# S5's sample end states and rotation tables made ahead of the S5 loop

## The chip, the cores and the metric

The kernel runs on one core of a Trainium2 chip. The metric is device time in microseconds (us) of one execution, as the median of several runs. The engines are TensorE (PE; its weight loads are PEld), VectorE (DVE), ScalarE (ACT), GpSimd (POOL) and SyncE (SP), which here issues all DMAs. Each works through its own queue of instructions in a fixed order, and an instruction that waits holds up everything behind it in its queue.

## The reference

One step of a decoder layer for a prompt of 512 tokens and a sample group of 8 sequences with 4 tokens each, width 1024, all in float32. After an RMSNorm, one projection feeds four branches: Mamba-2 SSD, S5 (a diagonal complex state space model), mLSTM, and cross-attention into 256 memory tokens. Each branch is projected down, weighted with a gate computed from the normed input, and summed; an output projection, a residual and a last norm follow.

What matters here is S5. It has 64 channel groups of 16 channels, each with a complex state of 64 values. With lam = exp(A dt) per state value,

    h[t] = lam * h[t-1] + B u[t],    y[t] = Re(C h[t]) + D u[t]

The prompt starts from h = 0. Each sample sequence starts from its own state h0, and its end state after four tokens is an output: lam^4 h0, plus what the four tokens add.

## The kernel before, in words

All large matmuls go through `unit` (L186 issues the matmuls): a 1024 x 128 slice of weights is loaded as `raw`, ScalarE rounds it to `whi` (L175), VectorE makes the rest `wlo` (L64, the line of all tensor_tensor operations), and TensorE adds up three products for eight blocks, 48 matmuls over 544 columns (512 prompt and 32 sample tokens). Their PSUM tile `pu` has two buffers; all other PSUM tiles share four banks, the tag "bk".

The order of work around the change is this.

- **Attention heads.** A generator `heads_` makes the prompt's attention for four heads, in eight steps: scores `psc` against the keys `krow`, softmax `prb`, transposes `ppt`, values `ppv`, and the branch's gate `zz`. The keys of head h lie in the tile `kst[h]`, which is not needed after the head's scores. A loop over the eight sample sequences b advances `heads_` by one step (`step(hd)`) and the S5 set-up `s5_setup` by two (`step(su, 2)`). Then POOL makes `pmx`, the sample's attention weights masked to sequence b, two loads bring `vb`, and TensorE adds into `pacc` (L675).
- **S5 set-up.** `s5_setup` is a generator with fourteen stops. It makes the powers of lam (`pwr`, `pwi`), the powers `pw8` for the rotations, the scaled B (`bbr`, `bbi`), the transposed C (`ctr`, `cti`) and the transposed states `h0`. Its scratch lies in the tile `merged`, which has no other use yet (`mflat` is its flat view).
- **Rotation tables.** For every two blocks of the loop, q = 0 to 3, `s5_rot(q)` makes on POOL the 64 powers of a unit complex number by doubling: two memsets, and in six rounds six elementwise operations on two halves, 36 operations on 8 to 256 columns, each needing the one before. The result goes to the first 512 columns of `st{q}`, a tile that shares its place with `kst[q]`. Table 0 is made after the heads, with scratch in `mflat`; tables 1 to 3 in the S5 loop after the blocks 0, 2 and 4, with scratch `rt` from the tags "sc1" and "sc2".
- **S5 loop.** For f = 0 to 7, 128 channels each: `s5_scan(f)` multiplies the inputs `U` by `bt` into two PSUM banks `pvr` and `pvi` (72 columns for each of four state blocks: 64 chunks of the prompt and 8 sample sequences), rotates by the table `E`, scans (L811, L812), rotates back, and copies the states into `hs`. At its end stand the end states of the samples, `hn`: lam^4 h0 by six operations on DVE for 32 columns, and two additions of the last eight columns of `pvr` and `pvi`. `s5_mats(f+1)` makes the next block's tables `bm` and `cm` on DVE and POOL, with scratch `q` in single buffers of the tags "sc1" and "sc2"; `s5_mats2(f+1)` transposes `bm` (`pbt`), multiplies to `pk` (L772) and sends the result through DRAM (`kd`, `tp`). `s5_y(f)` makes the outputs `py`, sends `yj` to DRAM (`yd`) and reads it back as `yt`; `s5_out` applies the GELU in the next round. `s5_in(f+2)` makes the inputs; its `uf` shares a buffer with `yj`. Steps of the generator `gate_down` put units on TensorE in between.
- **After the loop**, `hp` and `hn` are transposed (`pho`, `phq`) and written out.

The framework that builds the program fixes each engine's order at build time by the order of the code and by modelled times, and puts in the waits. So an instruction can stand earlier in its queue than in the code: of the six operations on `hn`, the first products of all eight blocks run before the loop, from 250.6 to 252.7 us.

Of the kernel before, what the change touches and what calls it, by code (L numbers as in the profile page):

```python
# [8 lines left out]
F32 = mybir.dt.float32  # L9
# [5 lines left out]
MUL, ADD, SUB, MAX, MIN = ALU.mult, ALU.add, ALU.subtract, ALU.max, ALU.min  # L15
# [19 lines left out]
def hybrid_kernel(ctx: ExitStack, tc: tile.TileContext, I, O):  # L35
# [12 lines left out]
    def bank(name="bk"):  # L48
        return pst.tile([P, 512], F32, name=name, tag="bk")

    def bc(ap, axis, n):
        ap = ap.unsqueeze(axis)
        shape = list(ap.shape)
        shape[axis] = n
        return ap.to_broadcast(shape)
# [7 lines left out]
    def tt(eng, out, a, b, op):  # L63
        eng.tensor_tensor(out, a, b, op)  # L64
# [4 lines left out]
    def cmul(e1, e2, outr, outi, ar, ai, br, bi, t1, t2):  # L69
        tt(e1, outr, ar, br, MUL)  # L70
        tt(e2, t1, ai, bi, MUL)
        tt(e1, outr, outr, t1, SUB)
        tt(e2, outi, ar, bi, MUL)
        tt(e1, t2, ai, br, MUL)
        tt(e2, outi, outi, t2, ADD)
# [158 lines left out]
    def step(gen, n=1):  # L234
        for _ in range(n):
            next(gen, None)
# [297 lines left out]
    def s5_setup():  # L534
# [102 lines left out]
            S.copy(h0[:, ri].rearrange("p b a -> p (b a)"), ph[:, 0:256])  # L637

        yield
        pd = bank("pd")  # L640
        T.transpose(pd[:, 0:8], sdg, ident[0:8, 0:8])
        V.tensor_copy(dcol, pd[:, 0:8])
# [2 lines left out]
    hd = heads_()  # L645
    pacc = pst.tile([P, 512], F32, name="pacc4", tag="bk")

    def s5_rot(q):
        er, ei = ev_[q][:, 0], ev_[q][:, 1]
        G.memset(er[:, :, :, 0:1], 1.0)  # L650
        G.memset(ei[:, :, :, 0:1], 0.0)
        for m in range(6):
            n = 1 << m
            if q < 1:
                ts_ = [mflat[:, (2 * q + i) * 256:(2 * q + i) * 256 + 8 * n] for i in range(2)]
            else:
                ts_ = [s5r.tile([P, 8 * n], F32, name="rt", tag=t) for t in ("sc1", "sc2")]
            t1, t2 = (t.rearrange("p (f a k) -> p f a k", f=2, a=4) for t in ts_)
            wm = tuple(bc(pw8[:, ri, m, 8 * q:8 * q + 8].rearrange("p (f a) -> p f a", a=4), 3, n) for ri in range(2))
            cmul(G, G, er[:, :, :, n:2 * n], ei[:, :, :, n:2 * n], er[:, :, :, 0:n], ei[:, :, :, 0:n], *wm, t1, t2)  # L660

    su = s5_setup()
    for b in range(NB):
        step(hd)
        step(su, 2)
        pm = xv.tile([P, 8, TS], F32, name="pmx", tag="qmx")
        tt(G, pm, pts.rearrange("p m (h t) -> p (m h) t", h=4), bc(bmask[:, b, :], 1, 8), MUL)
        vbs = []
        for m in range(2):
            vb = xv.tile([P, D], F32, name="vb", tag="vb")  # L670
            dma(vb, I["cache_mem_v"][0, b, m * P:(m + 1) * P].rearrange("p h d -> p (h d)"))
            vbs.append(vb)
        for m in range(2):
            for h in range(4):
                T.matmul(pacc[32 * h:32 * h + 32, 0:256], pm[:, 4 * m + h, :], vbs[m][:, h * 256:(h + 1) * 256],  # L675
                         start=b == 0 and m == 0, stop=b == 7 and m == 1, tile_position=(0, 32 * h))
    step(hd, 16)
    step(su, 4)
    stp = [cst.tile([P, 2, NT], F32, name=f"st{q}", tag=f"st{q}") for q in range(4)]
    stag = [stp[i // 2][:, i % 2] for i in range(NK)]  # L680

    ev_ = [t[:, :, 0:512].rearrange("p f (r a k) -> p r f a k", r=2, a=4) for t in stp]
    for q in range(1):
        s5_rot(q)
    os2 = xv.tile([P, 256], F32, name="os2", tag="pss", bufs=1)
    V.tensor_copy(os2, pacc[:, 0:256])
    pb = bank("pxo")
# [100 lines left out]
    def s5_scan(f, U, bt, E):  # L788
# [16 lines left out]
        tt(G, gr, gr, t1, ADD)  # L805
        tt(V, gi, E[:, 0], vi, MUL)
        tt(V, t2, E[:, 1], vr, MUL)
        tt(G, gi, gi, t2, SUB)
        for a in range(4):
            rb = rho8[:, 4 * f + a:4 * f + a + 1].to_broadcast([P, 64])  # L810
# [16 lines left out]
        for g2 in range(2):  # L827
# [2 lines left out]
            S.copy(hsv[64:128, :, g2, 9:73], t3[pr])  # L830
            for ri in range(2):
                S.copy(hsv[64 * ri:64 * ri + 64, :, g2, 0:8], h0[pr, ri, :, gs].rearrange("p b a -> p a b"))
        V.tensor_copy(hp[:, 8 * f:8 * f + 8], hs_[:, :, 72])

        p4 = (bc(pwr[:, 4, gs], 1, NB), bc(pwi[:, 4, gs], 1, NB))
        t1 = s5r.tile([P, NB, 4], F32, name="s1", tag="t1")
        t2 = s5r.tile([P, NB, 4], F32, name="s2", tag="t2")
        hnr, hni = hn[:, 0, :, gs], hn[:, 1, :, gs]
        cmul(V, V, hnr, hni, *p4, h0[:, 0, :, gs], h0[:, 1, :, gs], t1, t2)
        tt(V, hnr, hnr, vv[0][:, :, 64:72].rearrange("p a b -> p b a"), ADD)  # L840
        tt(V, hni, hni, vv[1][:, :, 64:72].rearrange("p a b -> p b a"), ADD)
        return hs_

    def s5_y(f, U, cm, tp, hs_):
# [38 lines left out]
    for f in range(8):  # L883
        bt, cm, tp, E = mt_
        hs_ = s5_scan(f, us_[f], bt, E)
        if f < 7:
            ma = s5_mats(f + 1)
        if f > 0:
            s5_out(f - 1, yt)
        step(gd)  # L890
        if f < 6:
            us_.append(s5_in(f + 2))
        if f < 7:
            mt_ = s5_mats2(f + 1, *ma)
        step(gd, (0, 1, 1, 1, 1, 0, 1, 1)[f])
        yt = s5_y(f, us_[f], cm, tp, hs_)
        if f % 2 == 0 and f // 2 + 1 in range(1, 4):
            s5_rot(f // 2 + 1)
    s5_out(7, yt)

    ph = bank("pho")
# [860 lines left out]
```

## Time and profile before

| | |
|---|---|
| Runs | 1478.04, 1473.43, 1478.48 us; median 1478.04 |
| Profiled execution | 1477.78 us, span 1476.0 us, mean granted clock 0.976 |
| Busy | PE 1397.2, PEld 1335.3, DVE 865.3, ACT 535.8, POOL 335.7 us |
| Attention heads with the set-up | about 157 to 255 us |
| S5 loop and its end | about 255 to 495 us |

Times in the profile count from the start of the span. A line of the profile names the code line, the engine, the operation, the output and inputs, and in brackets how long the engine had been idle before it and what ended that. A wait for several things is put down to the one that came last by the profile, which can be wrong. The granted clock is the share of TensorE's full clock that it was given.

### The profile page before, as it was taken

To read this page: it belongs to the slowest core of one execution; us is meant where nothing else is said; L and a number is where in the kernel's file an instruction comes from. 1 tells how busy PE (TensorE), PEld (TensorE's weight loads), DVE (VectorE), ACT (ScalarE), POOL (GpSimd) and SP (SyncE) were. 2 spreads that over 40 slices of the span, in tenths; PEclk is the share of its full clock that TensorE was granted. 3 is DMA by queue.
4 is the path that set the end of the run, shared out by engine and by line. 5 is a ranking of instruction groups with operands and counts; after the bars stand their busy time and mean duration, and the time that the engine had idled before them with its cause. 6 is when DMAs were issued, how large, how long until landed. Compare 5 with 4: busy or idle time off the path is not lost. (4 is left out here: it accounts for less than half of the span.)

```text
span 1476.0 us, 28630 instructions
## 1 busy us (share of the span) xinstructions
PE 1397.2 (95%) x11713; PEld 1335.3 (90%) x11713; DVE 865.3 (59%) x1682; ACT 535.8 (36%) x945; POOL 335.7 (23%) x511
## 2 busy tenths in 40 slices
PE   6999998979779899999999999999999999899997
PEld 6998887878768799999999989999999998789997
DVE  5455496676776594677777534544343465454553
ACT  4254233554445532433333422423233332114232
POOL 3010133676473011002222222000000011110222
PEclk9999999989989999999999999999999999999999
DMA  8577362545545323323222455222322235663341
GB/s 205 165 211 236 103 200 73 123 113 127 121 103 124 105 72 90 86 75 84 66 80 74 126 167 139 58 79 70 82 72 79 73 111 178 198 194 115 101 147 61
DMA packets 298884, 172.96 MB, mean 117 GB/s; under 512 B 46749, under 2 KB 289769, under 8 KB 298754
## 3 DMA queue, kind: packets, MB, share of 16 engines
q1 hardware_dynamic: 298754, 171.14, 42.1%
q8 instruction: 92, 1.51, 0.4%
q14 instruction: 38, 0.31, 0.1%
HBM read 145.35 MB, written 25.24 MB: 116 GB/s over the span
## 5 line engine op out<-in xcount | busy, mean ns | idle before, releaser
L186 PE MATMUL pu<-xh,whi 128*128 128x272 f32 (+1 forms) x2000 | 427.3, 292 | 0.2 <-DVE hp L949 0.2
L186 PE MATMUL pu<-xl,whi 128*128 128x272 f32 (+1 forms) x2000 | 425.6, 291 | 0.1
L186 PE MATMUL pu<-xh,wlo 128*128 128x272 f32 (+1 forms) x2000 | 425.1, 291 | 0.0
L64 DVE TENSOR_TENSOR wlo<-raw,whi 128x1024 fp32r<-128x1024 f32 x181 | 250.6, 1385 | 224.7 <-ACT whi L175 218.8
L175 ACT CAST whi<-raw 128x1024 fp32r<-128x1024 f32 x181 | 198.6, 1097 | 448.3 <-PE pu L186 343.7
L186 PEld LDWEIGHTS pu<-xh,whi 128*128 128x128 f32 x2000 | 319.0, 190 | 5.8 <-issue 3.9
L186 PEld LDWEIGHTS pu<-xl,whi 128*128 128x128 f32 x2000 | 319.4, 190 | 4.0 <-issue 3.3
L186 PEld LDWEIGHTS pu<-xh,wlo 128*128 128x128 f32 x2000 | 317.7, 190 | 3.3 <-issue 2.9
L186 PE MATMUL pu<-oh,whi 128*128 128x272 f32 x640 | 138.8, 298 | 5.8 <-ACT gt L215 5.8
L186 PE MATMUL pu<-ol,whi 128*128 128x272 f32 x640 | 138.8, 296 | 0.0
L186 PE MATMUL pu<-oh,wlo 128*128 128x272 f32 x640 | 136.1, 293 | 0.0
L186 PEld LDWEIGHTS pu<-oh,whi 128*128 128x128 f32 x640 | 104.7, 195 | 8.4 <-ACT gt L215 6.8
L186 PEld LDWEIGHTS pu<-ol,whi 128*128 128x128 f32 x640 | 105.2, 195 | 1.8 <-issue 1.6
L186 PEld LDWEIGHTS pu<-oh,wlo 128*128 128x128 f32 x640 | 103.6, 194 | 0.6 <-issue 0.4
L64 POOL TENSOR_TENSOR merged<-merged,gt 128x544 f32<-128x544 f32 x18 | 28.1, 1560 | 140.0 <-DVE gt L67 139.9
L67 DVE SCALAR_TENSOR_TENSOR cb<-cb,dcm,pcn 128x257 f32<-128x257 f32 x64 | 28.6, 478 | 25.9 <-PE pcn L1595 25.6
L186 PE MATMUL pu<-mh,whi 128*128 128x256 f32 x128 | 37.8, 295 | 0.1
L67 DVE SCALAR_TENSOR_TENSOR cc<-cc,dcm,pcu 128x257 f32<-128x257 f32 x24 | 11.4, 477 | 44.6 <-PE pcu L1474 44.6
L64 POOL TENSOR_TENSOR SS<-SS,dec 128x128 f32<-128x128 f32 x24 | 19.6, 816 | 77.6 <-DVE SS L1234 49.8
L186 PE MATMUL pu<-mlo,whi 128*128 128x256 f32 x128 | 37.1, 290 | 0.0
L186 PE MATMUL pu<-mh,wlo 128*128 128x256 f32 x128 | 36.2, 283 | 0.0
L1457 POOL MEMSET vtl<- 128x2 f32 x16 | 1.6, 100 | 143.0 <-PE pcu L1474 140.0
(636 smaller groups left out, 2224.1 us busy)
## 6 DMA issues: line engine op xcount, KB each, us to landing
raw<-in_w_in_dram SPq DMA_DIRECT2D x124, 512.0 KB
raw<-in_w_down_dram SPq DMA_DIRECT2D x32, 512.0 KB
kb<-in_cache_mem_k_dram SPq DMA_DIRECT2D x8, 1024.0 KB
raw<-in_w_mem_kv_dram SPq DMA_DIRECT2D x16, 512.0 KB
vb<-in_cache_mem_v_dram SPq DMA_DIRECT2D x16, 512.0 KB
cb<-in_state_mlstm_c_dram SPq DMA_DIRECT2D x16, 512.0 KB
out_dram<-cb SPq DMA_DIRECT2D x16, 512.0 KB
tp<-kd SPq DMA_DIRECT2D x16, 256.0 KB
```

The costliest lines, as they stand in the source:

```text
L64: eng.tensor_tensor(out, a, b, op)
L67: V.scalar_tensor_tensor(out, a, s, b, op0, op1)
L175: S.copy(hv, rv)
L186: T.matmul(ps[:, a, 0:c1 - c0], wt[:, k, :], xt[:, k, c0:c1], start=first, stop=last)
L1457: G.memset(vtl[:, 256:258].bitcast(F32), 0.0)
```

## The change

The products lam^4 h0 of all eight blocks are made at once in the set-up, on 256 columns, into `hn`: three operations on DVE and three on POOL. In `s5_scan` only the two additions stay, and they stand right after the four products from `pvr` and `pvi`, ahead of the scan. The copy of the prompt's end state `hp` moves from VectorE to ScalarE. All four rotation tables are made while the attention heads run: tables 0, 1 and 2 in the rounds b = 5, 6 and 7, ahead of `pmx`, table 3 after the loop, all with scratch in `mflat`. For that the set-up advances by three steps a round instead of two, and each `st{q}` is allocated when its table is made.

```diff
@@ s5_setup, after h0
+        p4 = (bc(pwr[:, 4, :], 1, NB), bc(pwi[:, 4, :], 1, NB))
+        n1, n2 = (s5b1[:, i * 256:(i + 1) * 256].rearrange("p (b a) -> p b a", b=NB) for i in range(2))
+        cmul(V, G, hn[:, 0], hn[:, 1], *p4, h0[:, 0], h0[:, 1], n1, n2)
+        yield
@@ heads
+    rt = mflat[:, 0:512]
+    stp, ev_ = [], []
     def s5_rot(q):
+        stp.append(cst.tile([P, 2, NT], F32, name=f"st{q}", tag=f"st{q}"))
+        ev_.append(stp[q][:, :, 0:512].rearrange("p f (r a k) -> p r f a k", r=2, a=4))
         er, ei = ev_[q][:, 0], ev_[q][:, 1]
...
-            if q < 1:
-                ts_ = [mflat[:, (2 * q + i) * 256:(2 * q + i) * 256 + 8 * n] for i in range(2)]
-            else:
-                ts_ = [s5r.tile([P, 8 * n], F32, name="rt", tag=t) for t in ("sc1", "sc2")]
+            ts_ = [rt[:, i * 256:i * 256 + 8 * n] for i in range(2)]
...
         step(hd)
-        step(su, 2)
+        step(su, 3)
+        if b > 4:
+            s5_rot(b - 5)
         pm = xv.tile([P, 8, TS], F32, name="pmx", tag="qmx")
...
     step(su, 4)
-    stp = [cst.tile([P, 2, NT], F32, name=f"st{q}", tag=f"st{q}") for q in range(4)]
+    s5_rot(3)
     stag = [stp[i // 2][:, i % 2] for i in range(NK)]
-    ev_ = [t[:, :, 0:512].rearrange("p f (r a k) -> p r f a k", r=2, a=4) for t in stp]
-    for q in range(1):
-        s5_rot(q)
@@ s5_scan
         tt(V, t2, E[:, 1], vr, MUL)
+        for ri in range(2):
+            e = hn[:, ri, :, gs]
+            tt(V, e, e, vv[ri][:, :, 64:72].rearrange("p a b -> p b a"), ADD)
...
-        V.tensor_copy(hp[:, 8 * f:8 * f + 8], hs_[:, :, 72])
-        p4 = (bc(pwr[:, 4, gs], 1, NB), bc(pwi[:, 4, gs], 1, NB))
-        t1 = s5r.tile([P, NB, 4], F32, name="s1", tag="t1")
-        t2 = s5r.tile([P, NB, 4], F32, name="s2", tag="t2")
-        hnr, hni = hn[:, 0, :, gs], hn[:, 1, :, gs]
-        cmul(V, V, hnr, hni, *p4, h0[:, 0, :, gs], h0[:, 1, :, gs], t1, t2)
-        tt(V, hnr, hnr, vv[0][:, :, 64:72].rearrange("p a b -> p b a"), ADD)
-        tt(V, hni, hni, vv[1][:, :, 64:72].rearrange("p a b -> p b a"), ADD)
+        S.copy(hp[:, 8 * f:8 * f + 8], hs_[:, :, 72])
@@ S5 loop
         yt = s5_y(f, us_[f], cm, tp, hs_)
-        if f % 2 == 0 and f // 2 + 1 in range(1, 4):
-            s5_rot(f // 2 + 1)
```

## The prediction

> **What bounds the kernel now.** I read the page's first part, then busy time by stage, then what TensorE waited for, and then the instructions around each wait, in order of time.
>
> ```profile
> span 1476.0 us, 28630 instructions
> PE 1397.2 (95%) x11713; PEld 1335.3 (90%) x11713; DVE 865.3 (59%) x1682; ACT 535.8 (36%) x945; POOL 335.7 (23%) x511
> ```
>
> TensorE is the bound: it is idle for 1476.0 − 1397.2 = 78.8 us, and only idle time, or matmuls run at a low clock, can be won. By stage (columns: stretch, length, busy us and count of PE, PEld, DVE, ACT, POOL; granted clock; DMA share; GB/s):
>
> ```profile
> 170.00:255.00 85.00, 81.03 (x618) 67.83 (x617) 64.15 (x211) 29.59 (x65) 30.87 (x64) 0.96 0.44 130
> 255.00:292.00 37.00, 35.41 (x325) 34.08 (x323) 25.96 (x40) 18.86 (x34) 21.38 (x36) 1.00 0.53 116
> 292.00:325.00 33.00, 22.56 (x246) 21.28 (x243) 24.49 (x42) 16.13 (x36) 27.26 (x35) 0.84 0.50 119
> 325.00:357.00 32.00, 28.71 (x291) 27.87 (x289) 21.46 (x41) 16.59 (x33) 20.97 (x44) 0.89 0.47 114
> 357.00:388.00 31.00, 23.30 (x254) 22.54 (x254) 25.56 (x41) 14.97 (x30) 18.01 (x19) 0.89 0.51 114
> 388.00:418.00 30.00, 26.69 (x272) 25.81 (x271) 17.15 (x36) 15.02 (x30) 19.05 (x42) 0.89 0.53 121
> 418.00:450.00 32.00, 24.73 (x333) 23.63 (x333) 26.43 (x42) 15.72 (x33) 17.99 (x20) 0.89 0.50 119
> 450.00:495.00 45.00, 35.27 (x398) 33.87 (x393) 29.01 (x70) 24.86 (x52) 12.12 (x23) 0.92 0.42 101
> ```
>
> The first row holds the attention heads, the others the S5 loop. TensorE idles 4.0 us in the heads and 1.6 + 10.4 + 3.3 + 7.7 + 3.3 + 7.3 + 9.7 = 43.3 us in the loop, over half of all its idle time. The cycles alternate: 10.4, 7.7 and 7.3 where a table of rotations has just been made, 3.3 in the two between. Its longest waits (total, times, longest):
>
> ```profile
> PE pk L772 <- ACT st L870: 7.7, 1, 7.7
> PE pk L772 <- DVE s L64: 7.3, 1, 7.3
> PE pk L772 <- ACT cm L753: 6.2, 3, 5.5
> ...
> PE phq L909 <- DVE hn L64: 3.2, 1, 3.2
> ```
>
> pk needs one of four PSUM banks, and pvr and pvi hold two of them until the end states have been added. The named releasers of the two longest waits are not the real ones; the instructions are:
>
> ```profile
> 381.19 1.08 PE L772 MATMUL pk<-cm,bbs 128*32 128x128 f32 x16 [7.70 <-ACT st L870]
> 380.79 0.19 DVE L64 TENSOR_TENSOR hn<-hn,pvi 128x32 f32<-128x32 f32 x1
> 442.34 1.08 PE L772 MATMUL pk<-cm,bbs 128*32 128x128 f32 x16 [7.27 <-DVE s L64]
> 441.90 0.19 DVE L64 TENSOR_TENSOR hn<-hn,pvi 128x32 f32<-128x32 f32 x1
> ```
>
> Both times pk starts 0.2 to 0.3 us after the addition that reads pvi last (380.79 + 0.19, 441.90 + 0.19). The second cause, on DVE:
>
> ```profile
> DVE q L64 <- POOL st L64: 13.8, 3, 6.7
> 304.25 1.59 DVE L64 TENSOR_TENSOR q<-pwi,bbr 128x512 f32<-128x512 f32 x1 [6.66 <-POOL st L64]
> ```
>
> s5_rot takes its scratch from the tags sc1 and sc2 of s5_mats, so the first product of the next group's tables waits for the last rotation, once per table 1 to 3, and the scan, the end states and pk behind it on DVE wait too.
>
> **The change part by part.** *Rotations out of the loop.* One table on POOL (columns: stretch, length, POOL busy and count, clock, DMA share, GB/s):
>
> ```profile
> 218.90:230.50 11.60, 10.91 (x36) 1.00 0.34 96
> 342.40:359.50 17.10, 15.84 (x36) 0.80 0.36 84
> ```
>
> Alone it takes 11.4 us; among the loop's work 17. Three tables, 34 us of POOL at the lone price, leave the loop with their 13.8 us of waits on DVE. What that gives TensorE lies between 0, where the stall only moves, and all of 25.4 us of the three cycles. I take the idle time of the cycles without a table as the floor: 25.4 − 3 × 3.3 = 15.5 us.
>
> *End states early.* In each group two multiplications and two subtractions on 32 columns go, 32 in the loop:
>
> ```profile
> 255.00:495.00 240.00, 5.99 (x32) 0.91 0.49 114
> ```
>
> That is 6.0 us of DVE, 0.75 a cycle, ahead of the additions that free the banks. The additions now stand right behind the four products from pvr and pvi, ahead of the scan. By itself this gives little in the old order, since the unit behind pk waits as well:
>
> ```profile
> 378.75 0.71 ACT L215 ACTIVATE gt<-pu,colH 128x544 f32<-128x544 f32 x1
> 379.42 1.22 DVE L64 TENSOR_TENSOR wlo<-raw,whi 128x1024 fp32r<-128x1024 f32 x1
> ```
>
> A pk at 373.5 would be followed by a matmul that needs the bank freed at 379.46: 1.7 us of the 7.7. So I count the banks inside the 15.5 and not again. The wait of phq (3.2 us) is for the last sum itself, which will be long done; the second phq waits for something else, so I take 2 of 0 to 3.2. The hp copies, eight short ones, move from DVE to ACT, which is busy 15 to 17 us of a cycle: nothing. If that cover were gone each would hold ACT's queue until the last hs copy, which stands ahead of it on ACT anyway.
>
> *Clock.* After a stall the matmuls run slowly. Granted clock in the 4 us after two loop stalls, and in the heads:
>
> ```profile
> 381.20:385.20 4.00, 4.00 (x31) 3.62 (x32) 3.21 (x7) 3.09 (x6) 0.00 (x0) 0.57 0.53 139
> 408.40:412.40 4.00, 3.25 (x25) 2.83 (x26) 2.82 (x7) 3.12 (x7) 4.00 (x10) 0.52 0.32 87
> 238.60:244.60 6.00, 5.95 (x34) 4.43 (x34) 2.08 (x6) 2.65 (x4) 0.00 (x0) 0.50 0.32 87
> ```
>
> Each stall so costs about 4 × (1 − 0.57) = 1.7 us more, 5 us for three. But the second row follows the short stall of a cycle without a table, so a stall at the floor still costs it. Of 0 to 5 I take 2.
>
> *The set-up and the tables in the heads.* The set-up advances three steps for a batch entry instead of two: the same instructions, earlier, on a DVE that is busy 64 of 85 us. The new product of lam^4 and h0 replaces sixteen multiplications by three on DVE and three on POOL, a gain on neither that counts. Where POOL's three further tables, 34 us, go:
>
> ```profile
> 180.06 5.43 POOL L64 TENSOR_TENSOR rho<-ecol,merged 128x32 f32<-128x32 f32 x1 [11.02 <-DVE merged L545]
> L64 DVE TENSOR_TENSOR pw<-pw,merged x12: 174/182/557, 198.6 to 208.7; 128x32 f32<-128x32 f32 x12
> 252.82 1.11 POOL L64 TENSOR_TENSOR q<-pwi,bbi 128x512 f32<-128x512 f32 x1 [21.18 <-PE ppv L501]
> 211.59 0.74 POOL L64 TENSOR_TENSOR pmx<-pts,bmask 128x256 f32<-128x256 f32 x1 [1.36 <-PE pacc L675]
> 228.53 0.42 PE L675 MATMUL pacc<-vb,pmx 128*32 128x256 f32 x4
> 219.93 0.75 POOL L64 TENSOR_TENSOR pmx<-pts,bmask 128x256 f32<-128x256 f32 x1
> 242.59 0.66 PE L675 MATMUL pacc<-vb,pmx 128*32 128x256 f32 x4
> ```
>
> The set-up's chain runs from 180 to the last power at 208.9, 29 us at two steps an entry; three steps would bring it to 199, and I take 202, as DVE is busy there. POOL idles for 21.2 us before the first S5 tables at 252.8: four tables and three masks from 202 end at 202 + 4 × 11.4 + 3 × 0.75 = 250, from 209 at 257. The masks pmx of the last batch entries now stand behind tables in POOL's queue; the attention sum pacc on TensorE waits for each, and on SP the next loads of vb, with weights behind them, wait for pacc. The last two stand behind two and three tables: from 202 they are made by 226 and 238, ahead of their uses at 228.5 and 242.6; from 209 they come 5 and 3 us late. That just holds. What may not be hidden is DVE:
>
> ```profile
> 225.01 6.04 DVE L67 SCALAR_TENSOR_TENSOR ol<-zz,oh 128x512 fp32r<-128x512 f32 x1
> 231.57 0.68 DVE L67 SCALAR_TENSOR_TENSOR ol<-zz,oh 128x512 fp32r<-128x512 f32 x1
> 238.65 1.11 PE L493 MATMUL ppt<-ident,prb 128*128 128x128 f32 x4 [3.97 <-DVE prb L488]
> ```
>
> While table 0 ran, one DVE instruction took 6.04 us instead of 0.68; the softmax behind it came late and TensorE stood 3.97 us, then ran 6 us at 0.50, 3 us lost: 7 us. In the loop, the row at 304.25, beside POOL's work, took 1.59 us, about 1 us lost if 0.68 is free for a like length. So three more tables cost the heads between 0 and 3 × 7 = 21 us. I take 6, about one such event: the loop's three tables show only the mild kind, and DVE still has idle time in the heads (64 of 85 us busy).
>
> The Trainium skill (SBUF — State Buffer, "Who interferes with whom") says that a VectorE instruction with two inputs in SBUF and a GpSimd instruction that reads SBUF exclude each other, the loser being blocked for the whole instruction of the other. The slow row has two such inputs, so the trace agrees in kind, but its 5.4 us are as long as many of POOL's instructions in a row. By the rule alone, a blocked instruction loses one POOL instruction, 0.7 us at the longest, which DVE's idle time would cover, and the sum would come out about 6 us lower, at 1458.
>
> **The sum**, against the profiled execution (span 1476.0, time 1477.78, so 1.8 outside; the median of the runs is 1478.04, no different): −15.5 − 2 − 2 + 6 = −13.5, a span of 1462.5 and a time of 1464.3. I say 1464.5.
>
> **The rivals.** *The loop has another limit.* For it:
>
> ```profile
> POOL uf L712 <- DMA yd<-yj: 13.3, 4, 6.2
> DVE t L64 <- POOL t L64: 11.2, 4, 5.2
> ```
>
> In the cycles without a table POOL waits for the store of yj, with the scan's products behind it, and the cycles are as long (30 and 32 us). If the order of the queues lets this bind everywhere, the three cycles win only the 1.7 us each, with 2 for phq: −7 + 6, 1477. Against it: those cycles do more matmul work (26.7 and 28.7 against 22.6 to 24.7 us).
>
> *The heads pay more than the loop wins.* One mechanism: POOL makes four tables in a row beside a DVE busy with heads, and each locks out DVE as table 0 did. 21 us, and 257 − 252.8 = 4 for the first S5 tables, less a loop gain of 13: +12, 1490. It decides once two or more further tables bring such an event. Against it stands the milder row in the loop.
>
> *Nearly all stalls go.* Banks free at once and tables ready: 25.4 + 5 + 3.2 = 33.6 off, 3 given back in the heads: 1447.
>
> That the change doesn't do what it says is small: the tags are single and the tables' tiles (those of the attention keys) come free head by head.
>
> **How the numbers follow.** Forecast (1457 to 1471) 0.48; another limit (1472 to 1480) 0.24; heads pay 0.13; nearly all stalls go (1443 to 1456) 0.15. The range 1450 to 1482 leaves out half of the last and most of the third. Half a per cent, 7.4 us, is what a measurement here tells from no change: faster, below 1470.6, holds nearly all the forecast and the last case, 0.60; same 0.27; slower 0.13.
>
> **What would show it.** Right: no POOL write of st after some 255 us; the DVE wait for st and both long pk waits gone; the idle of the three cycles near 3 us; pmx used without a wait. Wrong: DVE instructions of 3 us and more between 195 and 255, TensorE idle there above 12 us, or the loop's idle still near 43 us with yj, yt or hs as releasers.

## The result, and the profile after

The changed kernel takes 1484.56 us (median of six runs, 1482.23 to 1485.79) beside 1478.24 us for the kernel before on the same chip: a ratio of 1.0054, with an interval of 1.0038 to 1.0070. It is about 8 us slower, where 13.5 us less were forecast.

The first part of the page after:

```profile
span 1484.1 us, 28573 instructions
PE 1403.8 (95%) x11713; PEld 1342.0 (90%) x11713; DVE 862.5 (58%) x1629; ACT 535.5 (36%) x953; POOL 337.7 (23%) x514
```

TensorE does the same 11713 matmuls; it is idle for 80.3 us (78.8 before) and needs 6.6 us more for the matmuls themselves, at a lower clock.

To see where that arises, I cut both traces at the same two instructions: the first and the last of the eight rotations `gr<-st,pvr`, the first table product of a cycle of the loop. Groups of the tile pvr, of before and of after; the two times are the starts of the first and the last one:

```profile
L64 DVE TENSOR_TENSOR gr<-st,pvr x8: 405/410/421, 283.2 to 470.0; 128x256 f32<-128x256 f32 x8
```

```profile
L64 DVE TENSOR_TENSOR gr<-st,pvr x8: 408/414/418, 293.4 to 479.1; 128x256 f32<-128x256 f32 x8
```

The busy time by stage between these marks, of before and then of after (columns as in the prediction's stage windows):

```profile
170.00:283.20 113.20, 108.52 (x867) 94.42 (x866) 81.93 (x228) 44.86 (x92) 45.02 (x78) 0.97 0.44 124
283.20:470.00 186.80, 151.51 (x1676) 145.45 (x1675) 135.61 (x254) 93.47 (x189) 116.93 (x183) 0.90 0.51 120
```

```profile
170.00:293.40 123.40, 109.64 (x878) 96.33 (x877) 90.46 (x214) 41.97 (x86) 85.97 (x180) 0.94 0.39 115
293.40:479.10 185.70, 152.47 (x1643) 146.01 (x1642) 125.06 (x221) 94.72 (x198) 78.92 (x85) 0.87 0.50 118
```

The stretch up to the loop is 10.2 us longer, 9.1 of it idle time of TensorE (13.8 us in place of 4.7). The loop is 185.7 us in place of 186.8: with 38 us of POOL's work taken out of it and the long waits of pk and of VectorE's `q` gone, it is 1.1 us shorter. What follows the loop is 1005.0 us beside 1006.0. So 10.2 − 1.1 − 1.0 = 8.1, the difference of the spans.

**Ahead of the loop.** VectorE's two longest instructions there and the matmul that waited for the second, in order of time:

```profile
235.48 6.95 DVE L64 TENSOR_TENSOR hn<-hn,merged 128x256 f32<-128x256 f32 x1 [3.05 <-POOL merged L64]
248.72 6.73 DVE L488 TENSOR_SCALAR prb<-prb,xsc 128x256 f32<-128x256 f32 x4
254.71 1.97 PE L493 MATMUL ppt<-ident,prb 128*128 128x128 f32 x8 [11.34 <-DVE prb L488]
```

and the stretch right after, by stage:

```profile
255.00:260.00 5.00, 5.00 (x26) 5.00 (x25) 2.14 (x5) 3.07 (x3) 2.74 (x15) 0.56 0.01 3
```

The first is the subtraction of the new product lam^4 h0. It waits 3.05 us for its other half, which POOL makes at 234.70 in the midst of a table, and then lasts 6.95 us; the products of the same size that VectorE made before it, from 230.54 to 231.3, took 0.42 and 0.44 us. The attention head behind it in VectorE's queue is late by that, so its softmax scaling `prb` falls into the next table. Its four operations last 6.73 us together, 5.93 of them in a single one; an operation that isn't held takes 0.35. TensorE stands 11.34 us for it and then runs at a clock of 0.56.

**In the loop.** The same five stretches of time as in the prediction, in after. The loop begins 10.2 us later here, so they cut its cycles at another place:

```profile
292.00:325.00 33.00, 27.11 (x258) 25.14 (x257) 27.18 (x51) 15.36 (x30) 24.00 (x23) 0.79 0.46 110
325.00:357.00 32.00, 26.10 (x296) 24.76 (x294) 24.07 (x36) 16.89 (x36) 14.38 (x16) 0.97 0.57 131
357.00:388.00 31.00, 25.38 (x263) 24.72 (x264) 19.33 (x35) 15.07 (x32) 11.28 (x13) 0.89 0.51 116
388.00:418.00 30.00, 24.79 (x263) 24.13 (x261) 18.34 (x33) 13.61 (x28) 11.28 (x13) 0.90 0.51 119
418.00:450.00 32.00, 26.18 (x282) 25.48 (x284) 19.67 (x34) 17.08 (x36) 11.28 (x13) 0.87 0.49 113
```

The idle time was 10.4, 3.3, 7.7, 3.3, 7.3 before and is 5.9, 5.9, 5.6, 5.2, 5.8 now. From one `gr<-st,pvr` to the next it was 2.5, 8.8, 3.3, 7.7, 3.3, 7.3 and 2.4 us before and is 5.9, 0.0, 6.3, 5.3, 6.1, 5.0 and 4.8 now. So the alternation is gone, as a theory of tables and banks wants, but from the third cycle on all have met in the middle. What they wait for now (total, times, longest; TensorE from 255 to 495, the others from 292 to 450):

```profile
PE pu L186 <- ACT gt L215: 16.1, 3, 6.1
PE pk L778 <- ACT cm L759: 1.9, 3, 1.2
ACT st L872 <- DMA yt<-yd: 33.6, 5, 11.2
POOL uf L718 <- DMA yd<-yj: 29.9, 4, 8.3
DVE t L64 <- POOL t L64: 23.5, 5, 6.5
```

pk hardly waits any more, and VectorE's wait for POOL's last rotation has no row left. In their place stand three that all go back to y's way through DRAM. ScalarE's for yt was 8.2 us before:

```profile
ACT st L870 <- DMA yt<-yd: 8.2, 4, 2.9
```

One cycle of after in order of time shows how y holds the engines:

```profile
335.96 0.73 ACT L857 COPY yj<-py 128x288 f32<-128x288 f32 x2
342.07 1.80 SPq L860 DMA_DIRECT2D yd<-yj  x1
350.85 4.94 SPq L863 DMA_DIRECT2D yt<-yd  x8
350.94 0.12 POOL L718 MEMSET uf<- 128x32 f32 x1 [8.31 <-DMA yd<-yj]
351.84 1.31 DVE L64 TENSOR_TENSOR t<-t,t 128x256 f32<-128x256 f32 x1 [6.53 <-POOL t L64]
353.18 0.82 ACT L840 COPY hs<-t 64x256 f32<-64x256 f32 x2 [8.67 <-DVE t L64]
354.02 0.71 ACT L215 ACTIVATE gt<-pu,colH 128x544 f32<-128x544 f32 x1
354.79 0.66 PE L186 MATMUL pu<-oh,whi 128*128 128x272 f32 x2 [4.80 <-ACT gt L215]
```

yj is copied at 336; its store is issued at 342, behind the DMAs of kd, tp and raw in SyncE's queue, and has landed at 350.9. Until then POOL's memset of uf, which shares yj's buffer, stands, and with it the scan's products behind it, VectorE's sums, ScalarE's copies to hs, the gate `gt` behind them, and the matmul that needs the gate's PSUM buffer. ScalarE's next `st` finds yt there only at 355.2, 19 us after the copy of yj began. In the three cycles after this one that is the wait that ends last: yj is copied at 397.6, VectorE's sum is there at 414.1, but ScalarE still stands for yt, and the copies to hs and the gate stand behind it.

```profile
416.06 0.23 ACT L872 ACTIVATE st<-yt 128x32 f32<-128x32 f32 x1 [11.22 <-DMA yt<-yd]
418.09 0.71 ACT L215 ACTIVATE gt<-pu,colH 128x544 f32<-128x544 f32 x1
418.86 0.82 PE L186 MATMUL pu<-oh,whi 128*128 128x272 f32 x2 [6.07 <-ACT gt L215]
```

### The profile page after: what moved, and what is told of

It reads as the page before. It is cut to its first block, busy times and chain, and to the rows that moved or that the text cites. A ratio compares the mean times of both kernels' runs of the same rounds, so it can differ in the third digit from the quotient of the medians.

```text
span 1484.1 us, 28573 instructions
## 1 busy us (share of the span) xinstructions
PE 1403.8 (95%) x11713; PEld 1342.0 (90%) x11713; DVE 862.5 (58%) x1629; ACT 535.5 (36%) x953; POOL 337.7 (23%) x514
## 5 line engine op out<-in xcount | busy, mean ns | idle before, releaser
L67 DVE SCALAR_TENSOR_TENSOR cb<-cb,dcm,pcn 128x257 f32<-128x257 f32 x64 | 28.6, 478 | 26.0 <-PE pcn L1595 25.8
```

What stands on the lines that cost most here:

```text
L67: V.scalar_tensor_tensor(out, a, s, b, op0, op1)
```

## The experiments

Every kernel ran beside the kernel before on the same chip, and the ratios are to that. "Loop" is the time from the first to the last `gr<-st,pvr` of the profiled execution, 186.8 us before and 185.7 after; the part behind the last mark takes 995 to 1007 us in the profiled executions of all these kernels, so these marks say where time goes, and the medians how much.

### Each half of the change alone: e1 and e2

e1 is the kernel before with the end states alone, e2 the kernel after with the end states of before.

```diff
 e1, against before
+        cmul(V, G, hn[:, 0], hn[:, 1], *p4, h0[:, 0], h0[:, 1], n1, n2)
...
+            tt(V, e, e, vv[ri][:, :, 64:72].rearrange("p a b -> p b a"), ADD)
...
-        cmul(V, V, hnr, hni, *p4, h0[:, 0, :, gs], h0[:, 1, :, gs], t1, t2)
 e2, against after: the same lines the other way round
```

> The kernel before with the end states alone changed (lam^4 h0 in the set-up, sums right behind the four products, hp copied by ScalarE); set-up pace and the tables as before. Theory A (the loss is VectorE locked out of SBUF by POOL's tables in the heads, and the loop is held by yj's store in front of uf's memset): no further lockout, the pk waits gone, little won as yj's store then binds: 1473 to 1478. Theory B (the early end states bring the loss): 1481 or more.

> The changed kernel with the old end states (eight times six operations and the late sums on VectorE); the four tables in the heads and the set-up's quicker pace stay. Theory A: the lockouts in the heads stay and the pk waits return: 1483 to 1492. Theory B: 1474 to 1480.

Measured: e1 1476.37 us, ratio 0.9995 (0.9982 to 1.0008); e2 1477.07 us, 1.0007 (0.9993 to 1.0020). e1 lies in the range of theory A, e2 in that of theory B. So neither half costs anything by itself, and neither wins anything. That tables in the heads are dear by themselves, which I had held for likely in e2, fell. TensorE in the heads of e2:

```profile
170.00:255.00 85.00, 85.00 (x666) 72.36 (x664) 64.76 (x212) 31.25 (x65) 55.23 (x126) 1.00 0.44 132
```

It doesn't stand at all, with all four tables beside it. The stall in the heads needs both halves: the product with a part on POOL, and POOL full of tables. In the loop of e1 the waits of pk are gone and gt (13.5 us in three) and wlo (9.1 in two) wait instead; in e2 the waits of pk are back (30 us in five groups of releasers) and the loop is 185.8 us. In these four kernels, before, after, e1 and e2, the loop keeps its length (185.7 to 186.8 us) whichever wait is named.

### yj out of uf's buffer: e3 and e4

e3 is the kernel after, e4 the kernel before, with yj in the buffer of yt, so that POOL's memset no longer waits for the store.

```diff
-        yj = s5r.tile([P, 8, 72], F32, name="yj", tag="uf")
+        yj = s5r.tile([P, 8, 72], F32, name="yj", tag="yt")
```

> The changed kernel with yj in yt's buffer instead of uf's, so that POOL's memset of uf no longer waits for yj's store. Theory A: POOL's 30 us of waits for that store between 292 and 450 us and VectorE's 23 us behind them go; the loop gets 6 to 14 us shorter: 1470 to 1478. Rival C (the loop is held by something else, such as the read of yt on ScalarE): 1482 to 1486.

> The same buffer for yj in the kernel before. Theory A: only the cycles without a table waited for the store (13 us on POOL, 11 on VectorE), and TensorE stood 3.3 us in each: 1471 to 1477. Rival C: 1477 to 1480.

Measured: e3 1479.44 us, 1.0028 (1.0017 to 1.0038); e4 1478.81 us, 1.0019 (1.0005 to 1.0033). Some 4 us of the loss came back in e3 (loop 183.6), between the two expectations; e4, which lies in rival C's range, has no gain but a small loss (loop 190.6). POOL's wait is one part of y's hold. ScalarE's is the other, and it has grown, in e3:

```profile
ACT st L872 <- DMA yt<-yd: 39.3, 5, 12.2
```

### The stall in the heads: e5, e10 and e6

e5 takes the scaling `prb` off VectorE, e10 takes the product's half off POOL, e6 leaves the tables out (their rotations are by 1).

```diff
 e5
-                V.tensor_scalar(pr_[:, c, :], pr_[:, c, :], sc[:, 4 + c:5 + c], None, MUL)
+                S.activation(pr_[:, c, :], pr_[:, c, :], AF.Copy, scale=sc[:, 4 + c:5 + c])
 e10
-        cmul(V, G, hn[:, 0], hn[:, 1], *p4, h0[:, 0], h0[:, 1], n1, n2)
+        cmul(V, V, hn[:, 0], hn[:, 1], *p4, h0[:, 0], h0[:, 1], n1, n2)
 e6
-        for m in range(6):
+        G.memset(er[:, :, :, 1:64], 1.0)
+        G.memset(ei[:, :, :, 1:64], 0.0)
+        for m in range(0):
```

> The changed kernel with the softmax scaling prb of every head moved from VectorE to ScalarE (eight activations with a scale in place of eight tensor_scalars); nothing is left out. Theory A (the change loses its time at head 3, where VectorE's prb was locked out for 6.73 us each and TensorE then stood 11.34 us for it): the stall of TensorE ahead of head 3's ppt falls from 11.3 us to under 6 us (the locked-out hn product, 6.95 us, still makes VectorE late), the first table product of the loop starts 4 to 6 us earlier (288 to 290 us in place of 293.4), and the time is 1478 to 1482 us. Theory B (the time is lost to the queue on POOL, table 3 and all that stands behind it until 292.8 us, and the heads' stall is hidden by it): the stall shrinks but the first table product stays at 292 to 294 us, 1483 to 1486 us.

> The changed kernel with lam^4 h0 made by VectorE alone (all six operations of the product there, none on POOL); nothing is left out. Theory A (the product's POOL half stands between POOL's table operations: VectorE waits 3.05 us for it, is then locked out for 6.95 us, and head 3 comes late and into the next unbroken run of POOL): no wait of VectorE for POOL in the product, the stall of TensorE at head 3 is under 3 us as in the kernel with only the tables moved, the first table product at 286 to 290 us, 1474 to 1480 us. Theory B (any large VectorE work at this place collides with the tables, whoever makes its other half): one of the six VectorE operations or prb is again drawn out to 5 to 7 us, the first table product stays at 291 to 294 us, 1482 to 1486 us.

> The changed kernel with the rotation tables left out: two memsets per table stand in place of the 36 POOL operations that build it, so the rotations are by 1. All else, the early end states too, is as in the changed kernel. Theory A (the tables make the stall at head 3, but nothing in the loop): no VectorE operation of the heads is drawn out, TensorE's stall ahead of head 3's ppt is under 2 us, the first table product of the loop starts at 281 to 285 us, and the loop from first to last table product is still 183 to 187 us; 1472 to 1477 us. Theory B (the product alone makes head 3 late): first table product still at 290 us or later, 1481 to 1486 us.

Measured: e5 1475.27 us, 0.9988 (0.9974 to 1.0001); e10 1476.41 us, 0.9988 (0.9974 to 1.0003); e6 1465.10 us, 0.9919 (0.9893 to 0.9946). One letter in the product, or one operation on another engine, takes back the whole loss. TensorE's idle time ahead of the loop falls from 13.8 to 7.3 us in e10 and 8.1 in e5 (4.7 before), and the loops measure 182.7 and 178.8 us. Theory A had the mechanism, and for e5 too small a recovery; the first `gr` of e10, at 290.5, is just past its range. In e5 the subtraction of the product isn't held either (0.94 us), so e5 can't tell what the hold of `prb` cost from what that of the product did. The long instructions of VectorE have not gone, though. In e10 the product runs freely, and a `wlo` is hit; in e5 it is another `wlo`:

```profile
234.58 0.85 DVE L64 TENSOR_TENSOR hn<-hn,merged 128x256 f32<-128x256 f32 x2
249.91 7.26 DVE L64 TENSOR_TENSOR wlo<-raw,whi 128x1024 fp32r<-128x1024 f32 x1 [1.38 <-ACT whi L175]
```

```profile
221.70 5.15 DVE L64 TENSOR_TENSOR wlo<-raw,whi 128x1024 fp32r<-128x1024 f32 x1 [1.41 <-ACT whi L175]
```

What decides is who waits: a `wlo` is made a unit ahead of its use, and TensorE's longest wait between 170 and 292 us is then 4.8 us in e10 and 5.5 in e5, both for S5's first tables and inputs. In e6, without tables, no VectorE instruction of the heads goes over 2.4 us, and the first `gr` comes at 276.2, 7 us ahead of before; I had expected 281 to 285 and 1472 to 1477 us. Its loop is still 185.2 us, though POOL has nothing of the tables to do anywhere and the end states no longer hold the banks.

### The kernel before without tables in the loop: e7

Tables 1 to 3 are left out of the kernel before in the same way (rotations by 1); table 0 stays.

```diff
-        for m in range(6):
+        if q > 0:
+            G.memset(er[:, :, :, 1:64], 1.0)
+            G.memset(ei[:, :, :, 1:64], 0.0)
+        for m in range(6 if q < 1 else 0):
```

> The kernel before with tables 1 to 3 left out: two memsets in place of the 36 POOL operations of each of the three tables that were made inside the loop; table 0 stays. Theory A (the loop's length is set by the way of y through the memory and by the order of each queue, the tables were only what the waits were put down to): the loop from first to last table product is still 183 to 187 us (186.8 in the kernel before), 1473 to 1478 us. Theory B (the prediction's: the three table cycles cost the loop some 15 us): 170 to 175 us of loop, 1460 to 1466 us.

Measured: 1472.41 us, 0.9968 (0.9954 to 0.9982).

```profile
L64 DVE TENSOR_TENSOR gr<-st,pvr x8: 400/412/423, 280.2 to 464.2; 128x256 f32<-128x256 f32 x8
```

The loop is 184.0 us. This is the tables' half of the prediction's step, made pure: the three tables gone, at no price anywhere else. They are worth 2.8 us of loop. The late sums are still there, and pk still waits for its banks: in four cycles it starts 0.2 to 0.3 us after the addition that reads pvi last. Its waits are 32.1 us in seven times, in place of 26.2 in eight before (255 to 480 us); the longest group:

```profile
PE pk L775 <- ACT hs L832: 15.1, 2, 8.3
```

Both halves together are gone in e6, and its loop is 1.6 us shorter than before's, not 15.5. The median of e7 lies a little under theory A's range and far from theory B's.

### Moving the wait elsewhere: e16 and e22

yj takes the buffer of `bm`, in e10 and in the kernel before.

```diff
-        yj = s5r.tile([P, 8, 72], F32, name="yj", tag="uf")
+        yj = s5r.tile([P, 8, 72], F32, name="yj", tag="bm")
```

> The kernel with lam^4 h0 on VectorE alone (e10), and yj in the buffer of bm in place of that of uf; nothing is left out. So POOL's memsets of uf no longer wait for the store of yj, and bm, made half a cycle later, does. Theory A (the loop is held by y's way: POOL's wait for its store delays the scan, ScalarE's wait for its return delays gt and hs): POOL's wait uf<-yd (30 us in five) is gone, the first table product to the last takes 172 to 179 us in place of 182.7, and the time is 1466 to 1473 us. Theory B (one of the two waits is enough, ScalarE's for yt stays): the loop stays at 180 to 184 us, 1474 to 1478 us.

> The kernel before with yj in the buffer of bm in place of that of uf; nothing is left out and nothing of the change is in it. Theory A (y's way is one limit, tables and banks are the other, and in this kernel the other stays): the loop from first to last table product at 182 to 188 us, 1474 to 1480 us. Theory B (tables and banks never bind): 172 to 179 us of loop as with the change, 1464 to 1472 us.

Measured: e16 1478.66 us, 1.0009 (0.9997 to 1.0021), loop 190.1; e22 1483.75 us, 1.0041 (1.0025 to 1.0057), loop 202.7. Theory A is missed in both; e16 lies just above theory B, and e22 above every expectation. The products of bm now wait for the store, in e16 on two engines: 21.4 us in five times on VectorE and 23.1 in six on POOL (255 to 480 us). The half cycle of room that I had counted on was not there. The loops' lengths can't be compared with the others here, since more matmuls stand between the marks (1701 beside 1641 in e10, 1780 beside 1676 before); TensorE's idle time between them is 31.3 and 31.6 us, beside 32.3 in e10 and 35.3 before. So the wait was moved and not taken off. Why e22 is slower than the kernel before, these runs don't show.

### Without y's way: e20 and e21

The store and the eight loads are left out, and `s5_out` reads yj in place of yt, so the S5 outputs are in another order; yj takes the buffer of yt, which is free then, and POOL's memset has no store to wait for. e20 is e10 with this, e21 the kernel before with this.

```diff
-        yj = s5r.tile([P, 8, 72], F32, name="yj", tag="uf")
+        yj = s5r.tile([P, 8, 72], F32, name="yj", tag="yt")
...
-        yt = s5r.tile([P, 8, 72], F32, name="yt", tag="yt")
-        yd = s5d.tile([P, 8, 72], F32, name="yd", tag="yd")
-        dma(yd, yj)
-        for j in range(8):
-            dma(yt[:, j, :], bass.AP(tensor=yd.tensor, offset=yd.offset + j * 16 * 576, ap=[[72, 8], [576, 16], [1, 72]]))
-        return yt
+        return yj
```

> The kernel with lam^4 h0 on VectorE alone (e10) without y's way through DRAM: the store yd and the eight loads of yt are left out, and s5_out reads yj itself, so the S5 outputs are in another order. Theory A (y's way sets the loop's length once tables and banks are out of it): no waits uf<-yd and st<-yt, the loop from first to last table product 155 to 172 us in place of 182.7, 1450 to 1468 us. Theory B (something else, such as VectorE's own work of some 20 us a cycle or the low clock, sets it): 178 to 184 us, 1472 to 1477 us.

> The kernel before without y's way through DRAM: the store yd and the eight loads of yt are left out, and s5_out reads yj itself, so the S5 outputs are in another order. Theory A (tables and banks are the second limit of the loop): the waits of pk and of VectorE for the tables' last rotation come back as the longest, and the loop is 6 to 15 us longer than in the changed kernel without that way. Theory B (they cost nothing at all): the two loops within 3 us of each other.

Measured: e20 1437.57 us, 0.9722 (0.9701 to 0.9743), loop 149.0; e21 1459.66 us, 0.9880 (0.9864 to 0.9895), loop 177.6. Theory A of both holds in kind and is too small in size: e20 lies below its range, and the loops differ by 28.6 us, where 6 to 15 were expected. Without y's way the repaired change is worth 22.1 us. And in e21, from 255 to 480 us, the waits stand that the prediction had named, larger than ever:

```profile
PE pk L772 <- ACT uf L718: 17.6, 2, 8.8
```

```profile
DVE q L64 <- POOL st L64: 22.0, 3, 7.8
```

### An attempt that did not do what it should: e23 to e26

To keep y's way and take the waits off, e23 reads y back into the place of its finished rotation table and calls the GELU one cycle later. e24 adds a buffer for yj alone, for which the second rotation is rewritten, e25 is e24's edits in the kernel before, e26 is e24 with `prb` on ScalarE.

```diff
 e23, against e10
+        ga = stag[f]
         for j in range(8):
-            dma(yt[:, j, :], ...
+            dma(ga[:, c:c + w], ...
...
-        if f > 0:
-            s5_out(f - 1, yt)
+        if f > 1:
+            s5_out(f - 2)
```

> The kernel with lam^4 h0 on VectorE alone (e10), with y read back from DRAM into the place of its finished rotation table and the GELU one cycle later; nothing is left out. So ScalarE's queue meets yt only when it has long come, while POOL's memset of uf still waits for the store of yj. Theory A (each of the two waits holds a part): ScalarE's wait for the return of y (46 us in five) is gone, the loop from first to last table product at 165 to 178 us in place of 182.7, 1458 to 1472 us. Theory B (POOL's wait for the store alone sets the cycle): 180 to 184 us, 1474 to 1478 us.

> As the kernel with the GELU one cycle later (e23), and yj in a buffer of its own, for which the second rotation writes its products over gr and gi (two of its six operations change engine); nothing is left out. Theory A (y's way sets the loop only through the two queues it holds): both waits gone, the loop near the 149 us of the kernel without y's way, 150 to 162 us, 1440 to 1455 us. Theory B (the way itself takes DMA time or SP's queue and holds the loop all the same): over 165 us, 1460 us or more.

> The kernel before with the same two edits as e24 (GELU one cycle later from the table's place, yj in its own buffer), tables and end states left as they were before; nothing is left out. Theory A (tables and banks are the loop's next limit, worth what the prediction gave them or more): VectorE's wait for the last rotation and pk's waits are the longest, the loop 172 to 182 us, 1456 to 1466 us, 15 to 25 us above e24. Theory B (tables and banks do not matter even then): within 4 us of e24.

> e24 with the softmax scaling prb of the heads on ScalarE as in e5; nothing is left out. Theory A (a locked-out prb was the one costly event of the heads, and e10 had already cured it): no difference to e24 within 3 us. Theory B (a VectorE relieved of prb lets the heads end earlier): first table product 2 to 4 us earlier and 2 to 4 us faster than e24.

Measured: e23 1475.25 us, 0.9990 (0.9975 to 1.0006); e24 1473.59, 0.9979 (0.9965 to 0.9992); e25 1476.45, 0.9994 (0.9977 to 1.0012); e26 1472.16, 0.9968 (0.9954 to 0.9982). The times are those of theory B in e23 and e24, but they are no evidence for it: the wait that should have gone is there as before, in e23

```profile
ACT yt L870 <- DMA st<-yd: 46.6, 5, 11.2
```

because the order fixed at build time puts an instruction where its inputs are ready by modelled times, and so had put the GELU back to its old place: in e23 it stands on ScalarE at 350.17, right ahead of the copies to hs, as it does in e10 at 350.75. The model must have y back sooner than it comes; that is inferred. One thing e24 does show: POOL's wait for the store is gone there, ScalarE's for yt is 46.3 us in six, and the loop is 183.1 us beside 182.7 in e10. Taking off POOL's wait alone wins next to nothing there. e25 lies within 4 us of e24, as theory B has it, and is no evidence either, as ScalarE's wait stands in it too (25.3 us in seven). e26 against e24 is no more than 1.4 us, within what theory A allowed.

### The GELU forced behind py: e27 and e28

The scratch of the GELU now takes the buffer of hs, which is free only when py has been made. So it can't be moved ahead. yj has yt's old buffer to itself. e27 is e10 with this, e28 the kernel before with this; both compute everything.

```diff
         ga = stag[f]
-        t = s5r.tile([P, NT], F32, name="yt", tag="yt")
+        t = s5r.tile([P, NT], F32, name="yg", tag="hs")
...
-        yj = s5r.tile([P, 8, 72], F32, name="yj", tag="uf")
+        yj = s5r.tile([P, 8, 72], F32, name="yj", tag="yt")
...
-        if f > 1:
-            s5_out(f - 2)
...
         s5_y(f, us_[f], cm, tp, hs_)
+        if f > 0:
+            s5_out(f - 1)
```

> The kernel with lam^4 h0 on VectorE alone (e10), with y read back into the place of its finished rotation table, and the GELU of block f-1 forced behind the products py of block f, because its scratch takes the buffer of hs; yj has the buffer of yt, free now. Nothing is left out. In e23 and e24 the order fixed at build time had put the GELU back to its old place, so its wait for y's return stayed (46 us in five). Theory A (y's way holds the loop only through ScalarE's queue and POOL's memset): neither wait is left, the loop from first to last table product 150 to 165 us in place of 182.7, 1442 to 1458 us. Theory B (the way holds the loop by DMA time or SP's queue): 178 us or more, 1472 to 1478 us.

> The kernel before with the same edits as e27; tables and end states as they were before. Nothing is left out. Theory A (tables and banks are the next limit): pk's waits and VectorE's for the last rotation are the longest, the loop 172 to 182 us, 1456 to 1468 us, 12 us or more above e27. Theory B (tables and banks do not matter): within 4 us of e27.

Measured: e27 1443.81 us, 0.9781 (0.9758 to 0.9805); e28 1456.08 us, 0.9876 (0.9854 to 0.9898). Both lie in theory A's ranges, in time and in loop. e27 is 32 us faster than the kernel before, and the kernel after is 8 us slower than that. One way of y in e27, in order of time:

```profile
354.27 0.93 ACT L857 COPY yj<-py 128x288 f32<-128x288 f32 x2
355.10 0.75 ACT L870 ACTIVATE yg<-st 128x288 f32<-128x288 f32 x2
360.78 1.91 SPq L859 DMA_DIRECT2D yd<-yj  x1
368.58 5.00 SPq L863 DMA_DIRECT2D st<-yd  x8
```

and its stretches up to the loop and in it:

```profile
170.00:289.70 119.70, 112.17 (x895) 98.51 (x894) 85.22 (x219) 43.24 (x90) 85.57 (x178) 0.97 0.41 122
289.70:445.30 155.60, 142.82 (x1635) 136.28 (x1634) 129.68 (x217) 95.52 (x202) 83.64 (x83) 0.96 0.59 139
```

The way is as long as ever, 19 us from the first copy of yj to the end of the loads' issue, but hardly anything stands for it: the GELU at 355.10 reads the block before, ScalarE's wait for y is down to 5.1 us in two (292 to 450 us), and POOL's for the store is gone. The granted clock of the loop is 0.96 instead of 0.90. The same two rows of e28, and its two longest waits (TensorE, VectorE; 255 to 480 us):

```profile
170.00:280.80 110.80, 106.12 (x857) 92.03 (x856) 82.03 (x228) 43.56 (x86) 44.90 (x78) 0.98 0.43 125
280.80:456.00 175.20, 146.44 (x1664) 140.38 (x1663) 132.68 (x252) 93.12 (x193) 116.75 (x183) 0.91 0.53 127
```

```profile
PE pk L772 <- issue: 17.1, 2, 8.6
```

```profile
DVE q L64 <- POOL st L64: 20.6, 3, 7.0
```

So with y out of the queues the change, with the product on VectorE, is worth 12.3 us. TensorE's idle time in the loop falls from 28.8 to 12.8 us, by 16.0; ahead of the loop it grows from 4.7 to 7.5, by 2.8; the difference is about 13 us. The two profiled spans differ by only 8.6 us: the executions that were profiled took 1446.18 us in e27 and 1454.39 in e28, each some 2 us from its median, on opposite sides.

The four kernels side by side show two limits, each of which hides the other. TensorE's idle time in the loop is 35.3 us before. With tables and end states moved (e10) it is 32.3, with y out of the queues (e28) 28.8, with both (e27) 12.8: 3.0 and 6.5 us won one at a time, 22.5 together. How the gain with y out of the way divides between tables and banks was not tried.

## Why the prediction was wrong

The result lies 21.6 us above the forecast: 14.4 by the loop (−15.5 forecast, −1.1 measured), 4.2 by the stretch ahead of it (+6, +10.2), 3.0 by the terms for phq and the clock (−4 forecast, while what follows the loop is 1.0 us shorter).

**The loop's term, −15.5 us, is the step that failed.** It had two halves. That the waits of pk for the banks and of VectorE for the last rotation would go came true. That the three cycles would then sink to "the floor" of the cycles without a table did not: the loop gave 1.1 us. The floor was no floor. The cycles without tables were held by y's way, and they were as long as the others (30 and 32 us); a cycle rid of its tables came up against the same limit. The prediction had that rival, "the loop has another limit", with the right rows (`uf<-DMA yd`, `t<-POOL t`), and argued it away because those cycles did more matmul work. e7 shows what the tables alone were worth there, 2.8 us, and e6 what they were worth with the late sums, 1.6. In a loop in which y holds no queue the term has about the size that was forecast: 16.0 us of idle time from e28 to e27, 20.3 from e21 to e20. That 16.0 is so close to 15.5 is partly luck, as the term was 25.4 less a floor of 9.9 that y itself had made.

What I had not seen at all is ScalarE's wait for yt. It was 8.2 us before, short enough to be passed over, because another wait of ScalarE came first and covered it, that for VectorE's `q`, which stands behind the tables' last rotations (292 to 450 us):

```profile
ACT cm L746 <- DVE q L64: 23.8, 3, 10.7
```

It was not the stalls of pk that covered it: e1 has hardly any of them left (1.8 us) and 9.2 us for yt, while e7 still has them, without tables, and 42.7 us for yt. It is 33.6 us after.

**The end states: "a gain on neither that counts" is the second step that failed.** The product was costed at nothing because three operations on each engine are short. But it tied VectorE to a POOL that makes tables without a pause, at the one place where VectorE has TensorE's next operand to make. It cost 3.05 of waiting and 6.5 of being held (6.95 less 0.42), and with `prb` behind it 11.34 us of TensorE.

**The heads, +6 us, were mis-sized: 10.2.** "About one such event" was two, the second brought on by the first: in e10, where the product runs freely, the four operations of that `prb` take 1.91 us. The rival "heads pay" had the event right but its cause and its size wrong: three more tables alone bring no stall of TensorE (e2). The tables did come later than worked out: the first starts at 211.7, not 202 to 209, and the last of them is done at 294, not 250 to 257, as S5's own tables run in between.

**phq, −2:** as forecast, the 3.2 us wait for hn has no row left, and one of 4.4 for yj stays (4.1 before). Whether 2 us came of it the times don't show: the part behind the last mark is 1.0 us shorter, and it differs by more than that between executions. **The clock, −2,** had the wrong sign: 6.6 us more of busy time for the same matmuls. Of these 1.1 lie ahead of the loop, with its longer stall, 1.0 in the loop, whose clock is 0.87, not 0.90, though 33 fewer matmuls stand in it, and 4.0 behind the loop, where nothing was changed; those stay unexplained.

**What would show it.** Of the signs for "right", the waits of VectorE for st and of pk are gone and no row shows TensorE waiting for pmx, but tables are written until 294, and the three cycles stay at 5.6 to 5.9 us. Of those for "wrong", VectorE instructions of over 3 us appeared, TensorE's idle time between 195 and 255 us came to 11.3, just under the 12 named, and the loop's waits end with yj, yt and hs, while its idle time from 255 to 495 fell only from 43.3 to 36.8 us.

## What to carry to other kernels

A cycle that lacks the suspect and is as long as one that has it is not a floor but evidence of a second limit; look at what it waits for before its idle time is taken as what the others will fall to. Where two limits stand side by side, taking off either one wins little, and that is no proof that it costs nothing. A wait of a strict queue that is small now can be one that a larger stall covers: ask of each transfer how long its whole way is and which queue stands in front of its end. When work is moved beside a busy POOL, count not its length but what it ties together, and who waits for the engine that loses.

## What the runs showed that I had not expected

VectorE is held far longer than one instruction of POOL. In the changed kernel's heads these POOL rows stand around the two held instructions (each the start, the duration of the group and its size):

```profile
240.71 1.43 POOL L64 TENSOR_TENSOR st<-st,merged 128x256 f32<-128x256 f32 x2
242.10 1.00 POOL L64 TENSOR_TENSOR st<-st,pw 128x8 f32<-128x8 f32 x2
248.56 0.76 POOL L64 TENSOR_TENSOR st<-st,pw 128x128 f32<-128x128 f32 x2
253.11 1.40 POOL L64 TENSOR_TENSOR st<-st,merged 128x256 f32<-128x256 f32 x2
254.46 0.53 POOL L64 TENSOR_TENSOR merged<-st,pw 128x8 f32<-128x8 f32 x2
```

The subtraction of hn, begun at 235.48, ends at 242.43, just as POOL goes from the last round of one table to the first of the next. `prb` begins at 248.72, in the round of 128 columns, and its four operations end at 255.45, again just past the end of a table at 254.5. In between POOL ran a dozen instructions back to back, nearly all of 0.4 to 0.8 us. The two held `wlo` of e10 and e5 end in the same way, at 257.17 and 226.85, past the ends of a table at 255.2 and 224.8. VectorE instructions that began in the early rounds of 8 to 64 columns took their usual time or up to 1 us more. Not all that begin in the late rounds are held so long: a `wlo` of the changed kernel at 223.89, in the 256 columns of the first table, took 2.34 us, and e2 has four tables and no single VectorE instruction over 2.5 us between 170 and 293. The Trainium skill (SBUF — State Buffer, "Who interferes with whom") says that the one that comes second is blocked until the other's instruction is finished, and names `tensor_scalar` among the operations that can contend; the trace agrees on who is hit, but the 5 to 7 us are the rest of POOL's unbroken run and not one instruction of it. Why some are held and others not, and why the hold ends at the change of tables, I haven't tested.

Second, an order that is fixed at build time by modelled times defends itself. Moving the call of the GELU by a whole cycle changed nothing, presumably since the model has y back sooner than the 19 us that it takes; only a buffer that makes the early place impossible moved it, and e27 is 30 us faster than e24.
